# Choosing between two plans of expert slots at run time, and loading the last norm's vectors by DMA, in a hybrid encoder on one Trainium2 core

## Chip, cores and metric

The kernel runs on one core of a Trainium2 chip, as one launch. The metric is device time in microseconds, the median of several runs; lower is better. Everything below is float32, with matrix products of the dense layers split into high and low halves.

## What is computed

A trunk of two post-norm layers over 256 tokens of width 1024. Each layer has a hybrid mixer (a gated short convolution and a long convolution by Fourier transform) and then a channel mixer: dense SwiGLU in the first layer, a mixture of experts in the second. The change is in the second one's channel mixer and the norm behind it. Cut to what matters:

```python
def moe_swiglu(x, router, w1, w3, w2):          # 256 tokens, 8 experts of width 3584
    logits = xt @ router
    top_vals, top_idx = lax.top_k(logits, 2)
    top_w = jax.nn.softmax(top_vals, axis=-1)
    combine = einsum('tk,tke->te', top_w, one_hot(top_idx, 8))
    for e in range(8):
        y = y + combine[:, e:e+1] * ((silu(xt @ w1[e]) * (xt @ w3[e])) @ w2[e])

h = layer_norm(DEEPNORM_ALPHA * h + moe_swiglu(h, ...), ln_ffn_g[1], ln_ffn_b[1])
```

## The kernel before

The stream is held as 2 x 128 tokens on partitions, 1024 wide. Layer 0 and the mixer of layer 1 come first (to about 800 us); then the router, then the eight experts in a row, then the last norm and the output.

**Slots.** Only the tokens that chose an expert are computed for it. `posm` has each token's place within each expert; `one_hot` makes a matrix of tokens by slots from it, and `gather` multiplies it into the stream, which gives the expert's columns `xe`. An expert has 96 slots (wide) or 64 (narrow). Experts are taken by rank: rank 0 is always expert 0, whose key is set above all others, and the other seven follow by falling count. `vs` and `ix` hold the sorted keys and the expert numbers; SP loads the eight numbers into registers (line 1238), since the addresses of the weights depend on them. `RANKS` says which rank is computed at which place, and `N_WIDE = 5` makes ranks 0 to 4 wide: in the order of computing the experts are wide, narrow, wide, wide, narrow, wide, wide, narrow. `UNITS` says which experts share a gather. `cap` holds what each rank can take; `cmax` is how many tokens the fullest expert has beyond it. After the experts every engine loads that number (line 1266), and if it is above 0 (line 1297), `over` runs a loop over all experts for the tokens that are left.

**One expert.** `moe_run` works in four groups g of up to 1024 hidden columns. `up_proj` (matmuls on line 1054) multiplies by w1 and w3: the array is used as four column tiles of 32, a group of 32 slots in each, so 64 slots of w1 and of w3 take one PSUM bank each, and the 32 further slots of a wide expert a third bank. `gate` applies silu and the product, `turn` transposes, and `down_proj` (line 1103, and line 1108 for the further 32 slots) multiplies by w2. The down product of group g runs behind the up product of group g+1, across experts too. At the end the sum is copied from PSUM (line 1123), and `scatter` adds it to the stream `h_t`, weighted by `comb_r`. `hook` is called after each group: at group 1 it makes the next unit's one-hot matrix, at group 2 it gathers for it.

**Weights.** Each expert is 42 pieces of 1 MiB. `Weights` keeps a list of free buffers; `load` issues a DMA on SP's queue as soon as a buffer comes free, in the order of use (line 99). 16 buffers go round in the expert stage (11 named `wt`, 5 named `big`), and `W.extend` hands over a 17th, the place of `h_t`, once, in the residual ahead of the router. Because of that, `h_t` is filled with the scaled stream only in the first expert's group 1 (line 1172).

**The last norm.** `diag` builds diagonal matrices of the norm's scale and shift on POOL, `row_banks` sums them with a matrix of ones (line 523) so that every partition has the whole row, and ACT copies them out of PSUM. This happens within the last expert.

The scheduler of the framework sets the order of instructions on each engine ahead of time; instructions inside a conditional block stay inside it.

Of the kernel before, what the change touches and what calls it, by code (L numbers as in the profile page):

```python
# [33 lines left out]
RANKS = (0, 5, 1, 2, 6, 3, 4, 7)  # L34
N_WIDE = 5

UNITS = ((0,), (1, 2), (3, 4), (5,), (6, 7))
# [24 lines left out]
class Weights:  # L62
# [19 lines left out]

    def add(self, ap):

        self.src.append(ap)
# [4 lines left out]
    def load(self, upto=None):  # L90
        while self.free and self.nd < len(self.src) and (upto is None or self.nd < upto):
            a = self.free.pop(0)
            t = a[0]()
            if self.nd in self.halved:
# [119 lines left out]
def body(tc, nc, x, vec, rows, fg, winT, zT, fw1, fw2, fb, fw3, w_in, w_ao, w_ho, w_o, w13, w2,  # L214
# [105 lines left out]
    def of_rank(t, e, *q):  # L320
        if RANKS[e] == 0:
            return t[(0, *q)]
        return lambda: t[(ds(order[RANKS[e]], 1), *q)].rearrange("o p f -> (o p) f")

# [186 lines left out]

    def diag(i):

        t = big8([P, 2, KT, P])
        for q, v in enumerate((ln_g(i), ln_b(i))):
            nc.gpsimd.tensor_tensor(out=t[:, q], in0=v[:, :, None].to_broadcast([P, KT, P]),
                                    in1=id_s[:, None, :].to_broadcast([P, KT, P]), op=ALU.mult)
        return t

    def row_banks(t, q):  # L520
        banks = [acc_bank([P, 4, P]) for _ in range(2)]
        for hf in range(2):
            nc.tensor.matmul(banks[hf], ones_s, t[:, q, 4 * hf:4 * hf + 4], start=True, stop=True)
        return [b.rearrange("p k c -> p (k c)") for b in banks]
# [338 lines left out]
    for l in range(DEPTH):  # L863
# [12 lines left out]
        if l == 1:  # L876
            W.extend(lambda: hp.tile([P, 2048], F32, name="h_t", tag="h_t"), 1, False)
# [283 lines left out]
    pools = moe_pools(mctx)  # L1161
    oneh, xes, gts = {}, {}, {}

    def wide(e):
        return RANKS[e] < N_WIDE

    def hook(e, g):
        nonlocal h_t
        if e == 0 and g == 1:
            h_t = hp.tile([P, 2, D], F32, name="h_t", tag="h_t")  # L1170
            for tt in range(2):
                nc.gpsimd.tensor_scalar(out=h_t[:, tt], in0=hx[:, tt], scalar1=ALPHA, scalar2=None, op0=ALU.mult)
# [7 lines left out]
        if g == 1:  # L1180
            gts[e] = slots_T(pools, oneh.pop(e))
        if e == NE - 1 or g not in (1, 2) or unit_of(e) == unit_of(e + 1):
            return
        u = unit_of(e + 1)
        if g == 1:
            hot[u] = one_hot(pools, [(lambda tt, r=RANKS[q]: posm_r[:, tt, r:r + 1], slots(q)) for q in u])
        else:
            x = new_xe(pools, hot[u])
            for half in range(2):
                gather(x, hot[u], half)  # L1190
            hand_out(u, hot.pop(u), x)

    hot = {}

    def slots(e):
        return CAP if wide(e) else 64

    def unit_of(e):
        return next(u for u in UNITS if e in u)

    def hand_out(u, g, x):
        o = 0
        for e in u:
            oneh[e], xes[e] = g[:, :, o:o + slots(e)], x[:, :, o:o + slots(e)]
            o += slots(e)

    g0 = one_hot(pools, [(lambda tt: posm[:, tt, 0:1], CAP)])
# [3 lines left out]
    x = new_xe(pools, g0)  # L1211
    gather(x, g0, 0)
    gather(x, g0, 1)
    hand_out(UNITS[0], g0, x)
    with tc.issue_after(last["xv"].ins):

# [9 lines left out]
    def mt(shape, name, dt=F32):  # L1226
        return pools["mo"].tile(list(shape), dt, name=name, tag=name)


    cnt = rk[:, 2]  # L1230
    keys = mt([P, NE], "keys")
    nc.vector.scalar_tensor_tensor(out=keys, in0=cnt, scalar=float(NE), in1=iota_s[:, :NE], op0=ALU.mult, op1=ALU.subtract)
    nc.vector.memset(keys[:, 0:1], float(2 * NE * S))
    vs = mt([P, NE], "vs")
    ix = mt([P, NE], "ix", U32)
    nc.vector.max(out=vs, in_=keys)
    nc.vector.max_index(out=ix, in_max=vs, in_values=keys)
    for r, v in enumerate(nc.values_load_multi_w_load_instructions(ix[0:1], engines=[mybir.EngineType.SP], min_val=0,
                                                                   max_val=NE - 1)[1]):
        order[r] = v  # L1240
    perm, pick = mt([P, NE, NE], "perm"), mt([P, NE, NE], "pick")
    nc.vector.tensor_tensor(out=perm, in0=vs[:, :, None].to_broadcast([P, NE, NE]),
# [54 lines left out]
    with tc.If(count > 0):  # L1297
        over(0)
        with tc.If(count > CAP):
            over(CAP)  # L1300
# [98 lines left out]
```

## Time and profile before

| | us |
|---|---|
| median of 3 runs | 1699.12 (1696.47 to 1701.76) |
| profiled execution | 1701.1 |
| its span | 1699.3 |
| PE busy in the span | 1657.8 |
| DVE, ACT, POOL busy | 702.8, 489.5, 191.3 |
| share of 16 DMA engines, queue of the weights | 72.9% |

The span runs from the first to the last instruction of the program. A busy share is an average over stages that have different limits, so a stage is read by itself: by stretches, and by the times at which certain instructions start. PE's busy time includes matmuls whose ends are modelled. Waits, register loads and branches are not counted as busy; they are found by their lines.

### The profile page before, as it was taken

What the parts mean: (1) busy time and instruction counts of PE and PEld (TensorE: products, weight loads), DVE (VectorE), ACT (ScalarE), POOL (GpSimd) and SP (SyncE); (2) the same over time, 40 slices, a digit from 0 to 9 for tenths busy, and PEclk for the clock granted to TensorE, in tenths of its full rate; (3) what the DMA queues carried; (4) which work ended last, traced back from release to release, by engine and by line L of the source; (5) the groups of instructions that cost most, each with busy time, mean ns of one, the idle gap of its engine ahead of it and who ended that gap; (6) DMA issues with size and microseconds to landing.
All of it is one profiled execution on the core that took longest, in us unless ns stands there. A gap on an engine that the chain in (4) does not pass through costs nothing. (4 is left out here: it accounts for less than half of the span.)

```text
span 1699.3 us, 32630 instructions
## 1 busy us (share of the span) xinstructions
PE 1657.8 (98%) x14159; PEld 1081.0 (64%) x14159; DVE 702.8 (41%) x1013; ACT 489.5 (29%) x775; POOL 191.3 (11%) x163
## 2 busy tenths in 40 slices
PE   9799999999999999999999999999999999999996
PEld 7799999999998999998434333343343334434322
DVE  7789875775558898655200100101101011011102
ACT  5563575554545545542100101001001010010110
POOL 0635311030100443000010000000000000000000
PEclk9899999999999999999999999999999999999998
DMA  8442456355553536658689999999899999999993
GB/s 294 148 169 101 174 192 212 127 210 187 199 179 144 177 121 224 223 176 322 255 349 384 403 418 420 418 419 396 365 418 419 419 419 419 374 365 372 418 420 129
DMA packets 73581, 491.93 MB, mean 289 GB/s; under 512 B 8278, under 2 KB 13144, under 8 KB 14808
## 3 DMA queue, kind: packets, MB, share of 16 engines
q1 hardware_dynamic: 73000, 486.63, 72.9%
q0 software_dynamic: 432, 3.15, 0.5%
q8 instruction: 113, 1.85, 0.4%
q14 instruction: 36, 0.29, 0.0%
HBM read 488.70 MB, written 1.05 MB: 288 GB/s over the span
## 5 line engine op out<-in xcount | busy, mean ns | idle before, releaser
L1054 PE MATMUL mm<-wt,xe 128*32 128x512 f32 (+1 forms) x3664 | 473.0, 542 | 1.8 <-DMA wt<-in_m_dram 1.8
L174 PE MATMUL mm<-xh,hl 128*128 128x256 f32 x1376 | 390.7, 284 | 2.4 <-DVE t2k L747 2.3
L176 PE MATMUL mm<-xh,hl 128*128 128x256 f32 x1376 | 389.7, 283 | 2.3 <-DVE hl L168 2.3
L175 PE MATMUL mm<-xl,hl 128*128 128x256 f32 x1376 | 389.8, 283 | 0.1
L168 DVE TENSOR_TENSOR hl<-wt,hl 128x1024 fp32r<-128x1024 f32 x234 | 320.2, 1375 | 129.8 <-ACT hl L167 129.3
L1054 PE MATMUL mm<-big,xe 128*32 128x512 f32 (+1 forms) x1712 | 296.1, 535 | 0.0
L1054 PEld LDWEIGHTS mm<-wt,xe 128*32 128x32 f32 x3664 | 155.5, 110 | 214.6 <-issue 191.3
L167 ACT ACTIVATE hl<-wt 128x1024 fp32r<-128x1024 f32 x234 | 244.1, 1054 | 139.6 <-PE mm L176 74.3
L174 PEld LDWEIGHTS mm<-xh,hl 128*128 128x128 f32 x1376 | 264.1, 192 | 4.8 <-issue 2.9
L176 PEld LDWEIGHTS mm<-xh,hl 128*128 128x128 f32 x1376 | 264.0, 192 | 2.9 <-DVE hl L168 2.9
L175 PEld LDWEIGHTS mm<-xl,hl 128*128 128x128 f32 x1376 | 264.2, 192 | 1.5 <-DVE xl L168 0.7
L1064 DVE TENSOR_TENSOR act<-mm,act 128x512 f32<-128x512 f32 (+1 forms) x32 | 20.0, 625 | 486.4 <-PE mm L1054 486.4
L1103 PE MATMUL acc<-wt,at 128*32 128x512 f32 x1232 | 192.8, 593 | 0.0
L1054 PEld LDWEIGHTS mm<-big,xe 128*32 128x32 f32 x1712 | 86.3, 110 | 101.2 <-issue 90.5
L1063 ACT ACTIVATE act<-mm 128x512 f32<-128x512 f32 (+1 forms) x32 | 17.4, 544 | 459.9 <-PE mm L1054 459.9
L493 POOL TENSOR_TENSOR rs<-rs,mhalf 128x1 f32<-128x1 f32 x10 | 6.8, 676 | 1065.2 <-DVE rs L492 1065.2
L1103 PEld LDWEIGHTS acc<-wt,at 128*32 128x32 f32 x1232 | 53.2, 110 | 83.7 <-issue 81.7
L1103 PE MATMUL acc<-big,at 128*32 128x512 f32 x544 | 101.5, 593 | 0.6 <-DMA big<-in_m_dram 0.6
L1108 PE MATMUL acc<-wt,bt 128*32 128x512 f32 x352 | 100.2, 592 | 0.0
L174 PE MATMUL mm<-big,hl 128*128 128x256 f32 x256 | 72.3, 282 | 0.0
L176 PE MATMUL mm<-big,hl 128*128 128x256 f32 x256 | 72.3, 282 | 0.0
L175 PE MATMUL mm<-big,hl 128*128 128x256 f32 x256 | 72.3, 282 | 0.0
(251 smaller groups left out, 1803.0 us busy)
## 6 DMA issues: line engine op xcount, KB each, us to landing
wt<-in_m_dram SPq DMA_DIRECT2D x231, 1024.0 KB, 13.1
big<-in_m_dram SPq DMA_DIRECT2D x103, 1024.0 KB, 14.0
wt<-in_w_in_dram SPq DMA_DIRECT2D x62, 1024.0 KB, 4.8
wt<-in_w_dram SPq DMA_DIRECT2D x33, 1024.0 KB, 4.8
wt<-in_w_ho_dram SPq DMA_DIRECT2D x8, 1024.0 KB, 4.9
wt<-in_w_ao_dram SPq DMA_DIRECT2D x7, 1024.0 KB, 4.9
wt<-in_w_o_dram SPq DMA_DIRECT2D x6, 1024.0 KB, 4.9
big<-in_rows_dram POOLq DMA_DIRECT2D x3, 1024.0 KB, 5.6
```

The costliest lines, as they stand in the source:

```text
L167: a = nc.scalar.activation(hi, src, AF.Copy)
L168: v = nc.vector.tensor_tensor(out=lo, in0=src, in1=hi.bitcast(F32), op=ALU.subtract)
L174: nc.tensor.matmul(out, ah, bh, start=start, stop=False)
L175: nc.tensor.matmul(out, ah, bl, start=False, stop=False)
L176: nc.tensor.matmul(out, al, bh, start=False, stop=stop)
L493: last["pow"] = nc.gpsimd.tensor_tensor(out=rs, in0=rs, in1=mhalf[:, 0:1], op=ALU.pow)
L1054: nc.tensor.matmul(banks[r][32 * q:32 * q + 32, :n], xe[:, k, 32 * sg:32 * sg + 32], cols(w, b, q4), start=k == 0, stop=k == KT - 1, tile_ ...
L1063: nc.scalar.activation(a[:, :n], banks[0][:, :n], AF.Silu)
L1064: nc.vector.tensor_tensor(out=a[:, :n], in0=banks[1][:, :n], in1=a[:, :n], op=ALU.mult)
L1103: nc.tensor.matmul(ya[32 * q:32 * q + 32], at[:, f, 64 * b + 32 * sg:64 * b + 32 * sg + 32], ch[b][0][:, h * D + db * 512:h * D + (db + 1) ...
L1108: nc.tensor.matmul(yb[32 * q:32 * q + 32], bt[:, f, 32 * b:32 * b + 32], ch[b][0][:, h * D + db * 512:h * D + (db + 1) * 512], start=first ...
```

## The change

The one static plan is replaced by two. `LEAN` has ranks 1 to 4 wide and four narrow experts, expert 0 among them; `FULL` has ranks 0 to 5 wide. The number `lost`, how many tokens the fullest expert of `LEAN` would lose, is worked out ahead of the experts and loaded by every engine; `tc.If(lost < 1)` chooses. Each branch holds its own copy of the whole expert stage (`experts`) and its own copy of the state of the weights (`fork`); the test for left-over tokens and the loop `over` are now inside the `FULL` branch only. The first expert's gather stands ahead of the branch, into a buffer of the `big` pool; the weighting of tokens (`comb`) and the sorting of `posm` and `comb` by rank move behind it. `h_t` is no longer lent as a weight buffer. `diag` and `row_banks` go; the last norm's two vectors are read from HBM into every partition by a DMA on POOL's queue, into another buffer of `big`. The sort key of an expert is 8 times its count less its number, so no two are equal.

```diff
-RANKS = (0, 5, 1, 2, 6, 3, 4, 7)
-N_WIDE = 5
-UNITS = ((0,), (1, 2), (3, 4), (5,), (6, 7))
+LEAN = {"ranks": (0, 1, 5, 2, 6, 3, 4, 7), "wide": (1, 2, 3, 4), "units": ((0,), (1, 2), (3, 4), (5,), (6, 7))}
+FULL = {"ranks": (0, 6, 1, 2, 7, 3, 4, 5), "wide": (0, 1, 2, 3, 4, 5), "units": ((0,), (1, 2), (3, 4), (5,), (6,), (7,))}
...
+    def fork(self):
+
+        w = Weights(self.tc, self.nc, None, None, 0, 0)
+        w.src, w.raw, w.free = self.src, dict(self.raw), list(self.free)
+        w.nd, w.nu, w.whole, w.halved = self.nd, self.nu, self.whole, self.halved
+        return w
...
-        if l == 1:
-            W.extend(lambda: hp.tile([P, 2048], F32, name="h_t", tag="h_t"), 1, False)
...
+    x0 = big8([P, KT, S])[:, :, :CAP]
+    gbf = big8([P, 2, D])
...
+    def without(name, n, keep0):
+
+        cap = mt([P, NE], f"cap{name}")
+        nc.vector.tensor_scalar(out=cap, in0=keys, scalar1=vs[:, n:n + 1], scalar2=float(CAP - 64), op0=ALU.is_ge, op1=ALU.mult)
+        if not keep0:
+            nc.vector.memset(cap[:, 0:1], 0.0)
+        rest = mt([P, NE], f"rest{name}")
+        nc.vector.scalar_tensor_tensor(out=rest, in0=cnt, scalar=-64.0, in1=cap, op0=ALU.add, op1=ALU.subtract)
+        cmax, cmi = mt([P, 1], f"cmax{name}"), mt([P, 1], f"cmi{name}", I32)
+        nc.vector.reduce_max(out=cmax, in_=rest, axis=mybir.AxisListType.X)
+        nc.vector.tensor_scalar(out=cmax, in0=cmax, scalar1=0.0, scalar2=None, op0=ALU.max)
+        nc.vector.tensor_copy(cmi, cmax)
+        return cap, nc.values_load(cmi[0:1, 0:1], min_val=0, max_val=S)
+
+    lost = without("l", 4, False)[1]
+    nc.vector.max_index(out=ix, in_max=vs, in_values=keys)
+    gather(x0, g0, 0)
+    gather(x0, g0, 1)
...
-        if e == 0 and g == 1:
-            h_t = hp.tile([P, 2, D], F32, name="h_t", tag="h_t")
...
-        if e == NE - 1 and g == 0:
-            gb["diag"] = diag(N_LN - 1)
-        if e == NE - 1 and g == 2:
-            gb["last"] = big8([P, 2, D])
-            for q in range(2):
-                for hf, b in enumerate(row_banks(gb["diag"], q)):
-                    nc.scalar.activation(gb["last"][:, q, hf * 512:(hf + 1) * 512], b, AF.Copy)
...
+            if e == NE - 2 and g == 0:
+                src = rows[N_LN - 1]
+                nc.gpsimd.dma_start(gbf, bass.AP(tensor=src.tensor, offset=src.offset, ap=[[0, P], [D, 2], [1, D]]))
...
-    count = nc.values_load(cmi[0:1, 0:1], min_val=0, max_val=S)
...
-    with tc.If(count > 0):
-        over(0)
-        with tc.If(count > CAP):
-            over(CAP)
...
+    with tc.If(lost < 1) as plan:
+        with ExitStack() as pctx:
+            experts(LEAN, W.fork(), moe_pools(pctx))
+    with plan.Else():
+        with ExitStack() as pctx:
+            pools = moe_pools(pctx)
+            W1 = W.fork()
+            experts(FULL, W1, pools)
+
+            cap, count = without("f", 5, True)
+            with tc.If(count > 0):
+                over(pools, W1.free, cap, 0)
+                with tc.If(count > CAP):
+                    over(pools, W1.free, cap, CAP)
```

How instructions move, at three places. On PE, between the gather for the first expert and its first up products, before:

```order
L1009 MATMUL acc<-oneh,xh 128x96 x16
L1054 MATMUL mm<-big,xe 32x512 x4
L1054 MATMUL mm<-wt,xe 32x512 x4
L1054 MATMUL mm<-big,xe 32x512 x2
L1054 MATMUL mm<-wt,xe 32x512 x2
```

and now:

```order
L1002 MATMUL acc<-oneh,xh 128x96 x16
L1187 TENSOR_LOAD cmil
L1287 COMPARE_AND_BRANCH
L1047 MATMUL mm<-big 32x512 x4
L1047 MATMUL mm<-wt,big 32x512 x4
```

A register load and the branch (`cmil` is the number `lost`) stand between the two, and the up products read the gathered columns from a `big` buffer.

On SP, the weights that are issued ahead of the routing and the first ones behind it, before:

```order
L99 DMA wt<-in_m_dram 128x2048 x8
L99 DMA h_t<-in_m_dram 128x2048
L1238 TENSOR_LOAD ix
L1238 ISA x16
L1266 TENSOR_LOAD cmi
L1266 ISA x2
L99 DMA big<-in_m_dram 128x2048 x2
```

and now:

```order
L108 DMA wt<-in_m_dram 128x2048 x8
L1193 TENSOR_LOAD ix
L1187 TENSOR_LOAD cmil
L1287 COMPARE_AND_BRANCH
L108 DMA big<-in_m_dram 128x2048 x2
```

The load into `h_t` is gone, and the branch stands ahead of the first load that needs a buffer of the expert stage.

On POOL, from the norm ahead of the router to the end, before:

```order
L516 TENSOR_TENSOR big<-vec_s,id_s 128x1024 x2
L1218 TENSOR_TENSOR ew<-eb,ew 128x2
L1219 TENSOR_SCALAR ew<-ew 128x2
L1172 TENSOR_SCALAR h_t<-xh 128x1024 x2
L1266 TENSOR_LOAD cmi
L1297 COMPARE_AND_BRANCH
```

and now:

```order
L1187 TENSOR_LOAD cmil
L1287 COMPARE_AND_BRANCH
L1221 TENSOR_SCALAR h_t<-xh 128x1024
L1241 TENSOR_TENSOR ew<-eb,ew 128x2
L1221 TENSOR_SCALAR h_t<-xh 128x1024
L1242 TENSOR_SCALAR ew<-ew 128x2
L1224 DMA big<-in_rows_dram 128x2048
L1287 UNCONDITIONAL_BRANCH
```

The scaling of the stream (`h_t`) now stands ahead of and between the two steps of the tokens' weights (`ew`), the diagonals are gone, and the DMA of the norm's vectors is the next thing behind them.

## Rows read from the trace of the kernel before

**Rows 1.** The page, part 2: the TensorE clock granted, in tenths, 40 slices of 42.5 us.
```profile
PEclk9899999999999999999999999999999999999998
```

**Rows 2.** Timeline of PE, 818 to 822: start us, us, engine, line, operation, count.
```profile
818.62 1.06 PE L1054 MATMUL mm<-big,xe 128*32 128x512 f32 x8
```

**Rows 3.** Timeline of ACT: the first copies out of PSUM that end each expert.
```profile
950.96 1.21 ACT L1123 ACTIVATE y<-acc 64x512 f32<-64x512 f32 x2 [4.53 <-PE acc L1103]
...
1041.25 1.21 ACT L1123 ACTIVATE y<-acc 64x512 f32<-64x512 f32 x2 [2.84 <-PE acc L1103]
...
1163.97 1.21 ACT L1123 ACTIVATE y<-acc 64x512 f32<-64x512 f32 x2 [3.69 <-PE acc L1103]
...
1277.17 1.21 ACT L1123 ACTIVATE y<-acc 64x512 f32<-64x512 f32 x2 [2.93 <-PE acc L1103]
...
1372.35 1.21 ACT L1123 ACTIVATE y<-acc 64x512 f32<-64x512 f32 x2 [2.83 <-PE acc L1103]
...
1495.07 1.21 ACT L1123 ACTIVATE y<-acc 64x512 f32<-64x512 f32 x2 [3.69 <-PE acc L1103]
...
1608.28 1.21 ACT L1123 ACTIVATE y<-acc 64x512 f32<-64x512 f32 x2 [2.93 <-PE acc L1103]
...
1680.41 1.21 ACT L1123 ACTIVATE y<-acc 64x512 f32<-64x512 f32 x2 [10.02 <-PE acc L1103]
```

**Rows 4.** Timeline of PE in the first expert: eight instructions a row.
```profile
821.22 1.04 PE L1054 MATMUL mm<-big,xe 128*32 128x512 f32 x8
822.08 1.04 PE L1054 MATMUL mm<-wt,xe 128*32 128x512 f32 x8
```

**Rows 5.** Groups by form: the second down line, wide experts alone; count, busy us, ns.
```profile
L1108 PE MATMUL acc<-wt,bt 128*32 128x512 f32 x352 | 100.2, 592 | 0.0
...
L1108 PE MATMUL acc<-big,bt 128*32 128x512 f32 x200 | 68.3, 592 | 0.0
```

**Rows 6.** Stretches: length, busy us of PE, PEld, DVE, ACT, POOL, clock, DMA share, GB/s.
```profile
829.00:951.00 122.00, 121.91 (x1198) 43.88 (x1194) 9.02 (x19) 8.77 (x18) 5.52 (x2) 1.00 0.93 369
...
951.00:1041.00 90.00, 86.89 (x832) 30.59 (x824) 8.59 (x13) 7.50 (x14) 0.00 (x0) 1.00 1.01 419
...
1164.00:1277.00 113.00, 112.22 (x1084) 43.38 (x1084) 11.37 (x19) 9.45 (x18) 0.00 (x0) 1.00 0.95 390
...
829.00:1670.00 841.00, 830.54 (x7934) 316.11 (x7930) 82.76 (x146) 71.64 (x136) 5.52 (x2) 1.00 0.97 399
...
1670.00:1680.00 10.00, 10.00 (x96) 2.86 (x88) 0.00 (x0) 0.38 (x1) 0.00 (x0) 1.00 0.01 2
```

**Rows 7.** Line 523, the row sums of the diagonals: duration ns min/median/max, starts.
```profile
L523 PE MATMUL acc<-big,cst_s x8: 592/594/697, 1629.9 to 1637.2; 128*128 128x512 f32 x8
```

**Rows 8.** Lines 1266 and 1297, the test at the end: duration ns, starts us.
```profile
L1266 PEldq EVENT_SEMAPHORE  x6: 51/51/51, 1684.8 to 1685.3; - x6
...
L1266 PEldq TENSOR_LOAD <-cmi x1: 491/491/491, 1685.4 to 1685.4; - x1
...
L1297 PEldq COMPARE_BRANCH  x1: 3455/3455/3455, 1686.0 to 1686.0; - x1
...
L1297 DVEq COMPARE_BRANCH  x1: 72/72/72, 1687.3 to 1687.3; - x1
```

**Rows 9.** Timeline of SP's queue ahead of and behind the routing.
```profile
801.04 0.33 SPq L99 DMA_DIRECT2D h_t<-in_m_dram  x1
...
829.14 0.81 SPq L99 DMA_DIRECT2D big<-in_m_dram  x2
```

**Rows 10.** Tile h_t on POOL: duration ns min/median/max, starts.
```profile
L1172 POOL TENSOR_SCALAR h_t<-xh x2: 2765/2776/2786, 867.4 to 870.2; 128x1024 f32<-128x1024 f32 x2
```

**Rows 11.** The page, part 6: issues, KB each, us to landing.
```profile
wt<-in_w_in_dram SPq DMA_DIRECT2D x62, 1024.0 KB, 4.8
...
big<-in_rows_dram POOLq DMA_DIRECT2D x3, 1024.0 KB, 5.6
```

**Rows 12.** Timeline of DVE: the last norm begins; idle us ahead of it, releaser.
```profile
1687.97 1.88 DVE L488 BATCH_NORM_STATS2 st<-h_t 128x6 f32<-128x512 f32 x3 [0.65 <-DVEq L1297]
```

More of the change, by code (lines that the diff above doesn't have):

```diff
@@ L1160, in body, with mt @@
     mctx = ExitStack()
[L1161 to L1168, printed above, removed]
-        if e == 0 and g == 1:
-            h_t = hp.tile([P, 2, D], F32, name="h_t", tag="h_t")
-            for tt in range(2):
-                nc.gpsimd.tensor_scalar(out=h_t[:, tt], in0=hx[:, tt], scalar1=ALPHA, scalar2=None, op0=ALU.mult)
-        if e == NE - 1 and g == 0:
-            gb["diag"] = diag(N_LN - 1)
-        if e == NE - 1 and g == 2:
-            gb["last"] = big8([P, 2, D])
-            for q in range(2):
-                for hf, b in enumerate(row_banks(gb["diag"], q)):
-                    nc.scalar.activation(gb["last"][:, q, hf * 512:(hf + 1) * 512], b, AF.Copy)
[L1180 to L1207, printed above, removed]
+    first = {"mo": mctx.enter_context(tc.tile_pool(name="mo0", bufs=1))}
+    def mt(shape, name, dt=F32, pool=first):
+        return pool["mo"].tile(list(shape), dt, name=name, tag=name)
+    g0 = one_hot(first, [(lambda tt: posm[:, tt, 0:1], CAP)])
     with tc.issue_after(last["oneh"].ins), tc.issue_after(cp.ins):
@@ L1210, in body @@
             ins = h_half(tt, 1, back[tt])
[L1211 to L1215, printed above, removed]
+    x0 = big8([P, KT, S])[:, :, :CAP]
+    gbf = big8([P, 2, D])
+    cnt = mt([P, NE], "cnt")
+    nc.vector.tensor_copy(cnt, rk[:, 2])
+    keys = mt([P, NE], "keys")
+    nc.vector.scalar_tensor_tensor(out=keys, in0=cnt, scalar=float(NE), in1=iota_s[:, :NE], op0=ALU.mult, op1=ALU.subtract)
+    nc.vector.memset(keys[:, 0:1], float(2 * NE * S))
@@ new lines, in body, with experts, wide, slots @@
+    lost = without("l", 4, False)[1]
+    nc.vector.max_index(out=ix, in_max=vs, in_values=keys)
+    gather(x0, g0, 0)
+    gather(x0, g0, 1)
+    for r, v in enumerate(nc.values_load_multi_w_load_instructions(ix[0:1], engines=[mybir.EngineType.SP], min_val=0,
+                                                                   max_val=NE - 1)[1]):
+        order[r] = v
+    def experts(plan, W, pools):
+        ranks, units = plan["ranks"], plan["units"]
+        order["plan"] = plan
+        oneh, xes, gts, hot = {}, {}, {}, {}
+        posm_r, comb_r = mt([P, 2, NE], "posm_r", pool=pools), mt([P, 2, NE], "comb_r", pool=pools)
+        def wide(e):
+            return ranks[e] in plan["wide"]
+        def slots(e):
+            return CAP if wide(e) else 64
+        def unit_of(e):
+            return next(u for u in units if e in u)
+        def hand_out(u, g, x):
+            o = 0
+            for e in u:
+                oneh[e], xes[e] = g[:, :, o:o + slots(e)], x[:, :, o:o + slots(e)]
+                o += slots(e)
+        def hook(e, g):
+            if e == 0 and g == 1:
+                for tt in range(2):
+                    nc.gpsimd.tensor_scalar(out=h_t[:, tt], in0=hx[:, tt], scalar1=ALPHA, scalar2=None, op0=ALU.mult)
+            if e == NE - 2 and g == 0:
+                src = rows[N_LN - 1]
+                nc.gpsimd.dma_start(gbf, bass.AP(tensor=src.tensor, offset=src.offset, ap=[[0, P], [D, 2], [1, D]]))
+            if g == 1:
+                gts[e] = slots_T(pools, oneh.pop(e))
+            if e == NE - 1 or g not in (1, 2) or unit_of(e) == unit_of(e + 1):
+                return
+            u = unit_of(e + 1)
+            if g == 1:
+                hot[u] = one_hot(pools, [(lambda tt, r=ranks[q]: posm_r[:, tt, r:r + 1], slots(q)) for q in u])
+            else:
+                x = new_xe(pools, hot[u])
+                for half in range(2):
+                    gather(x, hot[u], half)
+                hand_out(u, hot.pop(u), x)
+        hand_out(units[0], g0, x0)
@@ L1237, in body @@
[L1237 to L1242, printed above, removed]
-                            in1=keys[:, None, :].to_broadcast([P, NE, NE]), op=ALU.is_equal)
```

68 lines of the change are left out of this document (21 added, 47 removed).

## The prediction

> **What bounds the kernel now.** The granted TensorE clock is full almost everywhere [rows 1], so the clock is no term. I first read where the expert stage begins and ends. The first expert matmul starts at 818.62 us [rows 2]; each expert ends with the first copy of its sum out of PSUM, eight rows in all [rows 3], the last at 1680.41; the tail from there to the end of the span (1699.3) is 18.9 us. So 862 of 1699 us are the expert stage, and nearly all of the change lies there.
>
> Then I asked who is the limit in it. Two resources are nearly even. **PE:** eight instructions (four column tiles, two passes each; a "unit") take 822.08 - 821.22 = 0.86 us [rows 4]. By the code a wide expert has 24 x 3 units of 512 columns and 8 x 3 half units up, and 14 x 3 down: 126 units; a narrow one has 84. The third that a wide one has more is 42 units, which the count of the second down line bears out: 552 instructions are 5 experts x 14 units x 8, a few records short [rows 5]. **DMA:** every expert brings 42 MiB. In the narrow expert's stretch the queue moves 419 GB/s, share 1.01, thus 2.50 us a MiB and 105 us an expert; in a wide one it falls to 390, in the first to 369, since no buffer is free [rows 6]. Over 829 to 1670 the mean is 399 GB/s. At 420 the same 335.6 MB would have taken 799 us, so 42 us of the queue were lost behind PE. Expert-to-expert times say the same [rows 3]: wide followed by wide 122.7 us, wide followed by narrow 113.2, narrow followed by wide 90.3, or 95.2 where a gather for the next unit lies in it; the first, wide, took 132.3 from 818.62. Wide ones are over the DMA's 105, narrow ones under it, and 16 MiB of buffers smooth it. PE is the limit through most of the stage.
>
> **Which plan runs.** The reference's own inputs send 61, 61, 71, 69, 67, 64, 53 and 66 assignments to the experts. Expert 0 has 61; the four largest others are 71, 69, 67, 66; the rest are 64, 61, 53. All fit (64 and 96 slots), the 64 with nothing to spare, so `lost` is 0 and the plan with four wide experts runs.
>
> **The change, part by part.**
> (a) Expert 0 becomes narrow and the order is now N W N W N W W N. 42 units x 0.857 = 36.0 us less on PE. To see whether the weights keep up I add up expert by expert, with the measured interval of the same kind. The first has 84 + 24 units to its end where it had 126 + 16: 132.3 - 34 x 0.857 = 103.2. Then 113.2, 95.2, 113.2, 95.2, 122.7, 113.2 (gathers stand in the same units as before, after the first, third, fifth and sixth expert).
> (b) The diagonal matrices and their row sums go: eight matmuls of 512 columns [rows 7], 8 x 0.43 = 3.4 us at PE's pace, at most 8 x 0.59 = 4.8; I take 4. They stood in the last expert, so 72.1 becomes 68.1. ACT and POOL lose work that nobody waited for.
> (c) The branch. On PE it is a TENSOR_LOAD behind the gather and a compare, and all expert matmuls are queued behind it. The same pair at the end of the kernel costs PE 0.49 us for the load and up to six 0.05 us waits ahead of it; the DVE compare took 0.07, but the jump that PE took there 3.46 [rows 8]. The lean plan is the fall-through, so I take 1.2 us: PE starts at 819.8. Bounds: 0 (the load runs while the gather drains) and 3.5. SP does its loads while no buffer is free and pays nothing: its queue stands from 801 to 829 [rows 9]. On DVE the chain of the largest count now comes ahead of the copies of x0; it is the one that stood there for the end's test, cost nothing then, and is in the 1.2 now.
> (d) POOL now scales the residual at the branch, 2 x 2.78 us [rows 10], ahead of the step that DVE's reciprocal waits for; the gates queue behind that reciprocal. 819.8 + 5.6 + about 3 for the small steps is 828.4; the first gate is due at 819.8 + 16 x 0.857 = 833.5. Hidden, with 5 us of cover; if it is gone, the excess is PE's.
> (e) h_t no longer takes the 17th MiB ahead of time [rows 9], and the last norm's rows come as 1 MiB on POOL's queue, right behind the reciprocal's step. Both go through the same 16 engines: 2 x 2.50 us if the DMA is the limit, 0 if PE is. Landing took 5.6 us and is needed 800 us later [rows 11].
>
> **The DMA beside it.** The first four buffers come free after 8 units instead of 12: 829.1 - 3.4 + 1.2 = 827. A lone MiB lands in 4.8 us [rows 11]. When the first expert ends, 50 MiB must be there, 16 were, one more is (e)'s: 831.8 + 34 x 2.5 = 916.8; then 105 each. PE alone against DMA alone: 923.0/916.8, 1036.2/1021.8, 1131.4/1126.8, 1244.6/1231.8, 1339.8/1336.8, 1462.5/1441.8, 1575.7/1546.8, 1643.8/1631.8. PE is later everywhere, by 3 to 29 us, under the 40 us that 16 buffers hold. But in the first, third and fifth expert the cover is 3 to 6 us, and weights are used in lumps of four; there PE will wait. I take 3 us in all; bounds 0 and 12 (4 at each).
>
> **The end.** DVE's idle 0.65 us ahead of the last norm [rows 12] is the test of the count, which goes. In its place DVE jumps over the general plan. The order has 79 instructions of DVE under the jump before and 266 now; DVE's jump before took 0.07 us, PE's, over 1229, took 3.46 [rows 8]. Between -0.65 and +2.9 I take 0: the distance is nearer to DVE's row. The Trainium skill ("Runtime: NRT & Kernel Launch", Instruction fetch mechanics) says that an engine fetches instructions in blocks of 256, and that a taken branch whose target lies outside the two blocks it holds has to wait for a DMA. The trace agrees on both jumps; by that rule this one may fall either way, and the time would be 1668.4 if it falls out.
>
> **Sum.** PE's end 1643.8 + 3 = 1646.8, tail 18.9: span 1665.7, where it was 1699.3. The profiled execution is 1.8 us longer than its span, 1701.1, and 2.0 above the median of 1699.1. So 1701.1 - 33.6 = 1667.5 for that execution, **1665.5** for the median. Another way: 36.0 + 4 - 1.2 - 3 = 35.8 less, thus 1663.3.
>
> **The rivals.**
> *Weights late.* The narrow experts starve and the DMA still idles behind the pair of wide ones. For it: both resources are within 1% of each other above. If half of the 42 us are lost again, the last MiB lands at 1631.8 + 21, and with the 10.4 us that PE had left after the DMA fell still [rows 6, 3] the span is 1682; time 1682. If all are lost again, 1703: no change. Against: the three stretches that lost most are the first wide one and the two pairs of wide ones, of which one pair is left.
> *The general plan runs* (the change doesn't do what it says). One assignment more at the expert with 64 decides it. Then six are wide, W N W W N W W W: 132.3 + 90.3 + 122.7 + 113.2 + 95.2 + 122.7 + 122.7 + 97.2 (68.1 + 34 units) = 896.3; with 819.8, 18.9 and 1.2 for the second test the span is 1736 and the time **1736**, slower. Against: the router's second and third logit differ by at least 0.0047 on every token in the reference, and no token near that would join that expert.
> *The branch is dear.* Every engine fetches anew at the entry and the end: 3.5 - 1.2 + 2.9 = 5.2 more, 1670.7. Inside the range.
>
> **How the numbers follow.** The sum's case, with the bounds of (b), (c), waits and jump, runs from 1658 to 1680: 0.82. Late weights, half: 0.10. Late weights in full, no change: 0.03. The general plan: 0.05. The range 1657 to 1682 leaves out the last two and part of the others. About 0.3%, 5 us, is what a measurement can tell from no change: faster 0.92, same 0.03, slower 0.05.
>
> **What would show it.** Eight endings with the first near 923, the last near 1647, and only 8/10 of the second down line's instructions (4 x 112 = 448); an SP queue that begins again near 827; the DMA share at 1.01 for all but the sixth and seventh expert; the first expert matmul at 819 to 821; a DVE gap ahead of the last norm of under 1 us or near 3.5. Wrong: over 660 instructions in that line (general plan), a first gate later than 836 (POOL's chain), or PE waits on weights over 12 us in sum.

## The result, and the profile after

The changed kernel took 1672.35 us (median of 4 runs, 1671.37 to 1673.24), beside 1698.61 for the kernel before on the same chip (1696.47 to 1701.76): ratio 0.9844, interval 0.9827 to 0.9861. The forecast was 1665.5, range 1657 to 1682. By the medians the gain is 26.3 us. Profiled execution against profiled execution it is 1672.95 (span 1671.2) where 1701.1 (span 1699.3) was: 28.1 us less by the spans, and 33.6 were forecast. So the direction came, and 5.5 us of the gain did not.

The eight endings of the experts stand in the timeline of ACT, as in [rows 3] (start us, us, engine, line, operation):

```profile
923.77 1.21 ACT L1116 ACTIVATE y<-acc 64x512 f32<-64x512 f32 x2 [2.85 <-PE acc L1096]
...
1035.90 1.21 ACT L1116 ACTIVATE y<-acc 64x512 f32<-64x512 f32 x2 [2.93 <-PE acc L1096]
...
1133.86 1.21 ACT L1116 ACTIVATE y<-acc 64x512 f32<-64x512 f32 x2 [2.85 <-PE acc L1096]
...
1245.94 1.21 ACT L1116 ACTIVATE y<-acc 64x512 f32<-64x512 f32 x2 [2.93 <-PE acc L1096]
...
1346.15 1.21 ACT L1116 ACTIVATE y<-acc 64x512 f32<-64x512 f32 x2 [2.84 <-PE acc L1096]
...
1468.91 1.21 ACT L1116 ACTIVATE y<-acc 64x512 f32<-64x512 f32 x2 [3.69 <-PE acc L1096]
...
1582.11 1.21 ACT L1116 ACTIVATE y<-acc 64x512 f32<-64x512 f32 x2 [2.93 <-PE acc L1096]
...
1650.99 1.21 ACT L1116 ACTIVATE y<-acc 64x512 f32<-64x512 f32 x2 [10.02 <-PE acc L1096]
```

They were forecast at 923.0, 1036.2, 1131.4, 1244.6, 1339.8, 1462.5, 1575.7, 1643.8. The intervals between them say more: 112.1, 98.0, 112.1, 100.2, 122.8, 113.2, 68.9. The two narrow experts in the middle, third and fifth, were to take 95.2 each. They took 2.8 and 5.0 more; the rest is within 2 us.

Where the stage begins (timeline of PE, as [rows 2]; the first row is the gather ahead of the branch):

```profile
815.18 3.71 PE L1002 MATMUL acc<-oneh,xh 128*128 128x96 f32 x32
818.82 1.06 PE L1047 MATMUL mm<-big 128*32 128x512 f32 x8
```

The first expert matmul starts at 818.82, where it was 818.62; the gather too is 0.2 later than before (814.98). The branch cost nothing at the entry. Which plan ran is read from the second down line, groups by form, as [rows 5]:

```profile
L1101 PE MATMUL acc<-wt,bt 128*32 128x512 f32 x288 | 76.8, 592 | 0.0
...
L1101 PE MATMUL acc<-big,bt 128*32 128x512 f32 x160 | 46.7, 592 | 0.0
```

448 = 4 x 112: four wide experts. The stretches (length; busy us of PE, PEld, DVE, ACT, POOL; clock; DMA share; GB/s), as [rows 6]:

```profile
829.00:938.00 109.00, 108.38 (x1016) 40.42 (x1009) 6.58 (x11) 10.89 (x19) 0.00 (x0) 1.00 1.01 420
...
1251.00:1347.00 96.00, 89.90 (x825) 32.56 (x824) 7.36 (x13) 6.21 (x13) 0.00 (x0) 1.00 1.01 419
1347.00:1467.00 120.00, 119.21 (x1152) 49.12 (x1154) 12.34 (x24) 9.51 (x19) 0.00 (x0) 1.00 1.00 411
1467.00:1579.00 112.00, 111.22 (x1076) 43.22 (x1072) 11.37 (x19) 9.30 (x18) 0.00 (x0) 1.00 0.96 393
...
829.00:1640.00 811.00, 795.93 (x7538) 304.74 (x7530) 76.94 (x132) 68.29 (x128) 0.00 (x0) 1.00 1.00 414
```

The queue moves 414 GB/s over the stage where it moved 399. It is at its pace up to the fifth expert and falls below it in the sixth (411) and the seventh (393), as forecast. It begins again at 825.06 (SP's queue, as [rows 9]; 827 was forecast):

```profile
825.06 0.83 SPq L108 DMA_DIRECT2D big<-in_m_dram  x2
```

The end, as [rows 12] (timeline of DVE; idle us in brackets):

```profile
1655.82 2.07 DVE L1134 SCALAR_TENSOR_TENSOR h_t<-mm,comb_r,h_t 128x512 f32<-128x512 f32 x3 [0.53 <-PE mm L1133]
1659.77 1.88 DVE L497 BATCH_NORM_STATS2 st<-h_t 128x6 f32<-128x512 f32 x3 [1.88 <-issue]
```

The compares of the branch, at the entry and at the jump behind the plan, as [rows 8] (line 1287: duration ns min/median/max, first and last start):

```profile
L1287 PEldq COMPARE_BRANCH  x2: 92/1920/3747, 817.8 to 1655.5; - x2
...
L1287 DVEq COMPARE_BRANCH  x2: 51/53/55, 819.9 to 1656.8; - x2
```

DVE's idle 0.65 us ahead of the last norm became 1.88: it jumps over the general plan. The compare that is put down for it takes only 0.05, but from it (1656.8) to the first instruction behind the jump (1659.8) it is 3.0 us; for 1.1 of them the last step of the scatter (the first row), already issued, still runs. PE's jump at the end takes 3.75 us, but nobody waits for PE there.

### The profile page after: what moved, and what is told of

It is laid out like the page before. It is cut to its first block, busy times and chain, and to the rows that moved or that the text cites. A ratio compares the mean times of both kernels' runs of the same rounds, so it can differ in the third digit from the quotient of the medians.

```text
span 1671.2 us, 31810 instructions
## 1 busy us (share of the span) xinstructions
PE 1621.3 (97%) x13769; PEld 1068.1 (64%) x13769; DVE 699.0 (42%) x1004; ACT 484.7 (29%) x766; POOL 188.3 (11%) x162
## 4 chain that ended last, share of the span: by engine, by line
PE 77%; DVE 9%; DMA 8%; ACT 2%; issue 2%; POOL 2%; SPq 0%; DVEq 0%; POOLq 0%; ACTq 0%
PE mm L1047 26%; PE acc L1096 10%; PE mm L183 8%; PE mm L184 8%; PE mm L185 8%; DMA wt<-in_m_dram 7%; DVE hl L177 3%; PE acc L1101 3%; PE acc L183 2%; PE acc L184 2%; PE acc L185 2%; PE acc L1002 1%; DVE big L177 1%; PE tp L1072 1%; PE mm L253 1%
## 5 line engine op out<-in xcount | busy, mean ns | idle before, releaser
L1047 PE MATMUL mm<-wt,xe 128*32 128x512 f32 (+1 forms) x3184 | 363.6, 541 | 0.5 <-DMA wt<-in_m_dram 0.5
L1047 PEld LDWEIGHTS mm<-wt,xe 128*32 128x32 f32 x3184 | 126.6, 110 | 194.8 <-issue 174.1
L1047 PE MATMUL mm<-big,xe 128*32 128x512 f32 (+1 forms) x1424 | 199.2, 538 | 1.3 <-DMA big<-in_m_dram 1.3
L1096 PE MATMUL acc<-wt,at 128*32 128x512 f32 x1200 | 178.5, 593 | 0.3 <-DMA wt<-in_m_dram 0.3
L1047 PEld LDWEIGHTS mm<-big,xe 128*32 128x32 f32 x1424 | 64.4, 110 | 74.9 <-issue 61.6
L1096 PE MATMUL acc<-big,at 128*32 128x512 f32 x592 | 95.9, 594 | 1.3 <-DMA big<-in_m_dram 1.3
L1101 PE MATMUL acc<-wt,bt 128*32 128x512 f32 x288 | 76.8, 592 | 0.0
```

The lines of the kernel that those rows point to most:

```text
L1047: nc.tensor.matmul(banks[r][32 * q:32 * q + 32, :n], xe[:, k, 32 * sg:32 * sg + 32], cols(w, b, q4), start=k == 0, stop=k == KT - 1, tile_ ...
L1096: nc.tensor.matmul(ya[32 * q:32 * q + 32], at[:, f, 64 * b + 32 * sg:64 * b + 32 * sg + 32], ch[b][0][:, h * D + db * 512:h * D + (db + 1) ...
L1101: nc.tensor.matmul(yb[32 * q:32 * q + 32], bt[:, f, 32 * b:32 * b + 32], ch[b][0][:, h * D + db * 512:h * D + (db + 1) * 512], start=first ...
```

## Experiments

Times of stages are best compared from the first expert matmul on, since everything ahead of it drifts by up to 1 us between executions. From there the changed kernel's last ending comes after 1650.99 - 818.82 = 832.2 us. All runs are beside the kernel before on the same chip.

**The norm's rows, late.**

```diff
+                with tc.issue_after(last["xv"].ins):
                     nc.gpsimd.dma_start(gbf, ...)
```

> The only edit: the DMA of the last norm's rows waits for the gather that the sixth expert makes, so its 1 MiB passes near 1440 us and not at 824. Theory A (weights are the limit to the fifth expert's end; DMA share 1.01 there): 1 MiB less ahead of it is 2.5 us, the fifth expert ends near 1343.7 (changed kernel 1346.15), the eighth near 1648.5 (1650.99), time near 1670. Theory B (PE with its gathers and lumps is the limit there): the endings stay within 0.5 us, time 1672.

1672.02 us, ratio 0.9842 (0.9825 to 0.9858). The timeline of POOL shows that the edit did not do what it says:

```profile
823.53 0.64 POOL L1225 DMA_DIRECT2D big<-in_rows_dram  x1
```

The transfer went out at 823.53, as early as before: the edit asks for a place in the list of instructions, and on POOL nothing stands ahead of it. So this is a second sample of the changed kernel and decides nothing; all eight endings agree with the first sample's within 0.1 us, counted from the first expert matmul (817.96).

**Five wide experts in the new frame.**

```diff
-LEAN = {"ranks": (0, 1, 5, 2, 6, 3, 4, 7), "wide": (1, 2, 3, 4), ...
+LEAN = {"ranks": (0, 5, 1, 2, 6, 3, 4, 7), "wide": (0, 1, 2, 3, 4), ...
```

> The lean plan gets the five wide experts and the order of the kernel before; branch, rows by DMA and the unlent h_t stay. Theory A (the gain is the 42 units of expert 0; the other parts give 4 us for the row sums and take 1.2 at the end): the first expert ends near 951, the last near 1677, time 1694 to 1698. Rival (the gain comes from the row sums, the earlier scaling of h_t or the new layout, and the narrow expert only starves): time 1672 to 1685.

1697.56 us, ratio 0.9991 (0.9982 to 1.0001). All the other parts together are worth 1.3 us, and their interval reaches no change; the fourth narrow expert is worth 25.2 us. The time that it spared PE was put at 36.0.

**No branch.** `LEAN` alone, no test, no general plan.

> The lean plan alone, with no branch and no general plan (left out: what happens when a token finds no slot). Theory A (the entry costs nothing, the jump at the end 1.2 us): the eight endings stay within 0.5 us, DVE's idle ahead of the last norm falls from 1.88 us to under 0.3, time about 1.5 us less, near 1671. Rival (the branch also costs inside the stage, by the order of instructions that the scheduler can't mix across it, or by code fetched twice): the endings move by 2 us or more.

1671.94 us, ratio 0.9839 (0.9823 to 0.9855). The branch as a whole costs 0.4 us, within what runs differ by, but this is a sum of two signs: the endings come 1.0 to 3.1 us later, as the rival said, and DVE's idle time ahead of the last norm is gone, as theory A said. The end is 2.1 us shorter (18.1 us from the last ending to the end of the span, where the changed kernel has 20.2). The start is 3.1 later (timeline of DVE, timeline of PE, and the columns of a stretch):

```profile
815.00 0.17 DVE L1242 RECIPROCAL ew<-ew 128x2 f32<-128x2 f32 x1 [1.82 <-POOL ew L1241]
...
815.82 0.17 DVE L974 SCALAR_TENSOR_TENSOR posm<-tp,mask 128x16 f32<-128x16 f32 x1
```

```profile
816.56 5.44 PE L1002 MATMUL acc<-oneh,xh 128*128 128x96 f32 x32 [1.73 <-DVE oneh L989]
821.92 1.06 PE L1047 MATMUL mm<-big 128*32 128x512 f32 x8
```

```profile
818.00:820.00 2.00, 2.00 (x12) 2.00 (x11) 1.90 (x8) 0.06 (x1) 2.00 (x1) 0.50 0.00 0
```

Without the branch the small steps of the gate weights move ahead of the routing in the list. DVE's reciprocal waits for POOL, which scales the residual for 2.80 us first, and `posm`, which the first gather needs, is queued behind the reciprocal. It is the wait that step (d) named, at another place: the branch keeps it behind the gather. Behind PE's idle 1.73 us the granted clock also falls to half (0.50 in the stretch shown, where the changed kernel has 1.00), and the gather takes 5.44 where it took 3.71. By the last ending only 1.0 of the 3.1 is left: the fifth expert waits less.

**The last norm inside both plans,** so that no engine jumps ahead of it.

```diff
+            last_norm()
     with plan.Else():
...
+            last_norm()
```

> The last norm and the stores are written into both plans, so DVE jumps after them and not before. Theory A (1.88 us of idle are the fetch behind the jump): the idle ahead of the norm falls under 0.3 us, the jump is paid beside the stores' landing, time 1.2 to 1.7 us less, near 1671. Rival (the jump is paid in full wherever it stands, since the closing barrier waits for every engine): the idle goes and the time stays at 1672.4, with a gap of 2 us or more behind the last store.

1674.93 us, ratio 0.9857 (0.984 to 0.9873). That is 2.6 us slower than the changed kernel, which neither theory said. DVE's idle time goes, and the stores start 2.3 us earlier (1662.25, where 1664.51 was); but the span ends at 1673.1, where it ended at 1671.2. Now SP jumps, behind the stores (lines 1299 and 1187: duration ns, first and last start):

```profile
L1299 SPq COMPARE_BRANCH  x2: 38/46/53, 818.0 to 1666.1; - x2
...
L1187 SPq FUSED_REGOPS  x1: 169/169/169, 1668.9 to 1668.9; - x1
```

Its compare is at 1666.1 and its next instruction 2.8 us later, at 1668.9; register operations behind the branch follow to 1671.6. In the changed kernel the same jump lies at 1625.4, 39 us ahead of the first store, and costs nothing. A jump is paid where its engine is the one that is waited for.

**The plans exchanged,** so that the jump comes at the entry.

```diff
-    with tc.If(lost < 1) as plan:
-        experts(LEAN, ...)
-    with plan.Else():
-        experts(FULL, ...)
+    with tc.If(lost > 0) as plan:
+        experts(FULL, ...)
+    with plan.Else():
+        experts(LEAN, ...)
```

> The two plans change places in the branch: the general plan stands first and the lean one is the other arm. Every engine now jumps at the entry over the general plan, and none jumps at the end. Theory A: a jump at the entry costs PE what its jump at the end cost, 3.75 us, and PE cannot hide it, since all expert matmuls stand behind it: first expert matmul at 822.2 to 822.6 instead of 818.82; DVE's idle 1.88 us ahead of the last norm goes; net +1.7, median 1674.1. Theory B: the jump hides behind the gather of the first unit: first expert matmul within 0.5 us of 818.8 and only the gain at the end is left, 1670.5.

1672.38 us, ratio 0.9842 (0.9826 to 0.9859): the same time, from two parts. The entry (timeline of PE, then two stretches) and the end (timeline of DVE):

```profile
815.36 3.71 PE L1002 MATMUL acc<-oneh,xh 128*128 128x96 f32 x32
821.95 1.74 PE L1047 MATMUL mm<-big 128*32 128x512 f32 x8 [2.88 <-issue]
```

```profile
822.00:824.00 2.00, 2.00 (x12) 0.65 (x16) 0.97 (x6) 0.00 (x0) 0.83 (x2) 0.55 0.08 16
824.00:826.00 2.00, 2.00 (x16) 0.70 (x12) 1.60 (x5) 0.00 (x0) 2.00 (x1) 0.60 0.00 0
```

```profile
1659.57 1.87 DVE L497 BATCH_NORM_STATS2 st<-h_t 128x6 f32<-128x512 f32 x3
```

The jump costs PE 2.88 us of idle time, and behind it the granted clock is 0.55 and 0.60 in two stretches of 2 us, a mixture of its two levels (1.2 and 2.4 GHz), where it is 1.00 in the changed kernel. The first ending comes 4.8 us later. So PE can't hide the jump, as theory A said, though the jump itself is shorter than its 3.75 us and the clock adds 1.7; theory A's time, 1674.1, did not come. The fifth expert then waits less for weights (98.4 us), so the last ending is only 2.8 later. At the end DVE has no idle time, and 3.0 us come back: 17.2 us to the end of the span. Not all of that is the jump. Behind the last ending PE waits 1.85 us for ACT in both runs, and then the granted clock falls: in the changed kernel within the next stretch of 2 us (1652.99 to 1654.99: 0.58), here later (1655.83 to 1657.83: 1.00), so the last scatter ends 6.9 us behind the last ending there and 5.8 here. This 1.1 comes and goes between executions (in the run with the late rows, a second sample of the changed kernel, the scatter ends after 5.9); the jump is the other 1.9, DVE's gap in the changed kernel. What the jump costs at one end it spares, nearly, at the other.

**Orders.** The pair of wide experts earlier:

```diff
+LEAN: N W N W W N W N   (units 0 / 1,2 / 3 / 4,5 / 6,7)    order a
+LEAN: N W W N W N W N   (units 0 / 1 / 2,3 / 4,5 / 6,7)    order b
```

> Lean order N W N W W N W N instead of N W N W N W W N; nothing else changes. Theory A (the narrow third and fifth experts waited for weights, 2.8 and 5.0 us, because they come when the queue is only some 6 us ahead): the pair of wide ones now comes as fourth and fifth and builds up cover before the next narrow one, so only the third still waits 2.8; intervals 112, 98, 122.7, 113.2, 95.2 or less, 113.2, 68 to 69; last ending about 1646.3, 4.7 us earlier than 1650.99, median 1667.7. Theory B (each narrow expert in the middle loses these microseconds by its own gathers and copies, wherever it stands): the sixth expert takes 98 to 100 us, the last ending stays at 1650 to 1651, median 1672.4. Theory C (the queue as a whole is the limit by now): last ending 1646 at best and the last landing at 1638, whatever PE does.

> Lean order N W W N W N W N. Theory A: the pair of wide ones comes second and third, and no narrow expert stands where the queue is short of cover; intervals 122.7, 113.2, 90 to 95, 113.2, 95.2, 113.2, 68.1; PE alone would end at 1643.5, the queue without a pause at 1638.2 for the last landing and so 1646.1 for the last ending (7.9 us from last landing to last ending as now): median 1667.5. Theory B: fourth and sixth take 98 to 100, median 1672.4. Theory D: the wide pair comes so early that all buffers fill and the queue pauses, which costs later: DMA share below 0.97 in the second or third expert, later narrow ones wait again, median 1671 to 1674.

Order a: 1669.75 us, ratio 0.9828 (0.9811 to 0.9844), last ending 829.6 us after the first expert matmul. Order b: 1669.30, ratio 0.9824 (0.9807 to 0.984), 828.9. Both gain about 3 us, and less than theory A said: the sixth expert, narrow, takes 97.9 us in both, near theory B's 98, though the last ending did not stay. The reason is in order b's fourth expert, narrow, with the last MiB that it needs landing 15.7 us ahead of its ending (at 1241.66, by the trace's record of the transfers; timeline of ACT):

```profile
1159.55 1.21 ACT L1116 ACTIVATE y<-acc 64x512 f32<-64x512 f32 x2 [2.93 <-PE acc L1096]
...
1257.37 1.21 ACT L1116 ACTIVATE y<-acc 64x512 f32<-64x512 f32 x2 [2.83 <-PE acc L1096]
```

1257.37 - 1159.55 = 97.8 us with only four short waits for weights, 1.1 us in sum: the same as the third expert of the changed kernel, in which no weight load waited for a DMA. So its 2.8 us are explained without the queue. What the two have in common is the gather for a unit of two experts, 160 columns. The third expert of the changed kernel against the fifth of the kernel before (groups by form, line of the gather; count, busy us, ns, idle):

```profile
L1002 PE MATMUL acc<-oneh,xh 128*128 128x160 f32 x32 | 5.7, 315 | 0.7 <-DVE oneh L989 0.7
...
L1002 PEld LDWEIGHTS acc<-oneh,xh 128*128 128x128 f32 x32 | 4.5, 189 | 4.3 <-issue 2.5 <-DVE oneh L989 1.0 <-ACT xe L1006 0.8
```

```profile
L1009 PE MATMUL acc<-oneh,xh 128*128 128x96 f32 x32 | 4.3, 282 | 0.4 <-DVE oneh L996 0.4
...
L1009 PEld LDWEIGHTS acc<-oneh,xh 128*128 128x128 f32 x32 | 3.8, 191 | 2.3 <-issue 1.7 <-DVE oneh L996 0.6
```

160 columns cost 1.4 us more of matmuls and 2.0 more of idle time ahead of their weight loads. The 95.2 us came from an expert with a gather of 96 columns. Order a shows that the queue stands just behind: its third expert gathers only 96 columns and takes 97.7 us all the same, now with 3.8 us of waits for weights. Theory D is borne out in part: the queue pauses at the early wide pair (1049 to 1142: 383 GB/s), but the next narrow expert, the sixth, doesn't take longer for it (97.9 us).

**The general plan, always.**

```diff
-    with tc.If(lost < 1) as plan:
+    with tc.If(lost < 0) as plan:
```

> The test is made so that the general plan always runs (six wide, two narrow, then its own test of the count, which finds nothing over). Theory A, the rival as the prediction priced it: eight intervals 132.3, 90.3, 122.7, 113.2, 95.2, 122.7, 122.7, 97.2, time 1736. Theory B: PE's taken jump at the entry comes on top, 3.7 us: 1740. Theory C: with six wide ones the queue always has cover and PE takes less than its measured intervals: below 1731.

1735.20 us (1734.44 to 1735.90), ratio 1.0214 (1.0197 to 1.0231). Theory A, the rival's sum of 1736, within 1 us. The page has no compare at that line (presumably since a count below 0 can't be, and the test is folded away), so this run says nothing of the entry's jump. It is what the changed kernel costs where one token more comes to an expert than the lean plan has slots, less the jump at the entry, which would come on top as in the exchanged plans.

**Gathers in the wide experts,** the order kept.

```diff
-"units": ((0,), (1, 2), (3, 4), (5,), (6, 7))
+"units": ((0,), (1,), (2, 3), (4, 5), (6, 7))
```

> The order of the changed kernel, but the gathers for the next unit lie in the wide experts (units 0 / 1 / 2,3 / 4,5 / 6,7), so that the narrow third and fifth carry none. Theory A (the queue is the limit up to the fifth expert; a narrow one ends 5.9 us after its last weights land, however little PE has to do): third and fifth still end near 1133.9 and 1346.2, nothing is gained, median 1671.5 to 1672.8; PE's waits for weights grow by what the gathers took. Theory B (the third expert's 2.8 us over the forecast are its own gather of 160 columns, 97.9 us against 95.2 with 96 columns, and PE's time counts): third and fifth shorter by 7 to 10 us, median about 1660.

1671.73 us, ratio 0.9837 (0.9821 to 0.9854): theory A. Third and fifth expert end 315.0 and 527.3 us after the first expert matmul, as in the changed kernel, to 0.1 us. What PE was spared went into waiting for weights, 18.9 us in all, where the changed kernel has 9.0 (waits of the weight loads over the stage: us, times, longest):

```profile
PEld mm L1047 <- DMA wt<-in_m_dram: 6.5, 10, 2.3
PEld acc L1096 <- DMA wt<-in_m_dram: 4.5, 7, 1.6
PEld mm L1047 <- DMA big<-in_m_dram: 4.5, 4, 2.2
...
PEld acc L1096 <- DMA big<-in_m_dram: 3.4, 4, 2.3
```

So two limits stood one on the other in the third expert: PE with its gather, and the queue, which would have let it end no earlier.

**A 17th MiB ahead, and the rows truly late.**

```diff
     gbf = big8([P, 2, D])
+    W.extend(lambda: gbf.rearrange("p a d -> p (a d)"), 1, False)
...
+                nc.vector.tensor_copy(gbf[:, 0, 0:1], xes[e][:, 0, 0:1])
                 src = rows[N_LN - 1]
```

> The buffer of the norm rows holds a 17th MiB of weights first, loaded with the others before the stage, and the rows come only when the seventh expert begins (a copy of one column from its gathered tokens into that buffer holds them back). Theory A (the two MiB of term (e) cost the queue's pace as long as the queue is the limit): every landing up to the fifth expert comes 2.5 us earlier against the first expert matmul; rows of the fifth expert's waits fall from 8.4 us of weight-load idle time to under 6; last ending 2.5 earlier, median 1669.9. Theory B (PE is the limit again by the end, and the queue was late only in passing): no change, 1672.4.

1668.04 us (1667.74 to 1669.14), ratio 0.9817 (0.9801 to 0.9834), the fastest of all. The fifth and the last ending (timeline of ACT), and the waits of the weight loads over the stage:

```profile
1341.31 1.21 ACT L1116 ACTIVATE y<-acc 64x512 f32<-64x512 f32 x2 [2.85 <-PE acc L1096]
...
1646.52 1.21 ACT L1116 ACTIVATE y<-acc 64x512 f32<-64x512 f32 x2 [10.02 <-PE acc L1096]
```

```profile
PEld mm L1047 <- DMA wt<-in_m_dram: 2.6, 5, 1.3
...
PEld mm L1047 <- DMA big<-in_m_dram: 1.3, 2, 1.0
...
PEld acc L1096 <- DMA wt<-in_m_dram: 1.0, 4, 0.3
...
PEld acc L1096 <- DMA big<-in_m_dram: 0.6, 2, 0.3
```

The 17th MiB goes out at 805.41, and the rows at 1414.6. The last ending comes 828.0 us after the first expert matmul (818.50), 4.15 us less than 832.2, where theory A expected 2.5: the edit moves both MiB of step (e), and the landings up to the fifth expert are 4.3 to 4.5 us earlier by the same count, nearly two MiB at 2.5. Waits for weights fall from 9.0 us to 5.5. This is the price of step (e), and most of what the forecast missed.

**Order b with the gathers in the wide experts, and both together.**

> Order N W W N W N W N with the gathers in the wide experts (units 0 / 1 / 2 / 3,4 / 5,6 / 7). PE's intervals by the rows so far: 104, 122, 115, 88, 115, 88, 115, 69, some 12 us less than in the same order with gathers in the narrow ones. Theory A (floor of the queue): 319 MiB from 832 on at 2.527 us, last landing 1638.2, last ending 7.9 behind it, 1646: median 1667. Theory B (PE counts): last ending 1636, median 1657. Theory C (gathers cost the same wherever they lie): 1669.3 as with this order before.

> Both edits together: order N W W N W N W N, gathers in the wide experts, a 17th MiB of weights ahead and the norm rows late. Theory A (floor of the queue): 318 MiB from 832 on, 2.5 us less than with the order and the gathers alone, about 1664.5. Theory B (PE is the limit): the same time as without the 17th buffer.

The first took 1669.50 us (ratio 0.9826, 0.9809 to 0.9842), the last ending after 828.3 us: 0.6 less than order b alone. A gather of 160 columns costs a wide expert less than a narrow one: the third, wide, takes 117.6 us with it and 113.2 without, the fourth, narrow, 90.5 without and 97.8 with it. But this plan has six units instead of five, so one gather more, of 64 columns, lies in the seventh expert: it takes 116.4 us where order b has 112.1, with 0.5 us of waits for weights. And the queue pauses in the third expert (1049 to 1142: 380 GB/s), and the last one, with 5.5 us of waits for weights, takes 70.7 us instead of 68.9. These two take back nearly all that the narrow experts gain. The time is theory C's, but not for its reason.

The second took 1671.33 (0.9835, 0.9818 to 0.9851): 3.3 us slower than the 17th MiB alone and 1.8 slower than the order alone (there the runs overlap), against both theories. The 17th MiB's lead is lost in the third expert, where all buffers are full (366 GB/s in the same stretch), and the rows go out in the fifth, when the queue is the limit (timeline of POOL):

```profile
1325.56 0.64 POOL L1226 DMA_DIRECT2D big<-in_rows_dram  x1 [500.91 <-POOLq L1289]
```

The last landing that the fifth expert needs comes 4.2 us later than without the 17th MiB, counted from the first expert matmul, and the sixth expert, narrow, takes 94.6 us instead of 90.4. The rows' own MiB is 2.4 us of this; the other 1.8 are there already at the fourth expert's last landing, and why is not shown. Here a lead was worth what it kept until the first wait, and it kept nothing through a stretch in which the queue stood.

## Why the prediction was right, and where it fell short

Added up in its own terms, from the first expert matmul on:

| step | forecast us | measured us |
|---|---|---|
| first expert | 103.2 | 104.95 |
| second and fourth | 2 x 113.2 | 2 x 112.1 |
| third | 95.2 | 98.0 |
| fifth | 95.2 | 100.2 |
| sixth, seventh | 122.7, 113.2 | 122.8, 113.2 |
| last, (b) in it | 68.1 | 68.9 |
| waits for weights, in all | 3 | in the rows above |
| stage | 827.0 | 832.2 |
| (c) start | 819.8 | 818.8 |
| tail | 18.9 | 20.2 |
| span | 1665.7 | 1671.2 |

The start, 1.0 us early, and the tail, 1.3 late, nearly cancel, which is luck; the stage is the miss.

**(a)** The mechanism is right: one wide expert less, and the run with five wide ones shows that nearly the whole gain is this. Its size failed at two points of the sum. The interval 95.2 was taken for both narrow experts "where a gather for the next unit lies in it", whatever the gather's width: with 160 columns it is 98.0, and order b shows that with hardly a wait for weights. And **"I take 3 us in all"** was too little: the fifth expert alone took 5.0 us over its 95.2, with the gather of 96 columns that the 95.2 has. The waits of its weight loads, 8.4 us in sum, not all of which holds up the matmuls:

```profile
PEld acc L1096 <- DMA big<-in_m_dram: 2.9, 2, 2.2
PEld mm L1047 <- DMA big<-in_m_dram: 2.9, 2, 2.2
...
PEld mm L1047 <- DMA wt<-in_m_dram: 1.4, 1, 1.4
PEld acc L1096 <- DMA wt<-in_m_dram: 1.2, 1, 1.2
```

The prediction held PE's ending against the last landing and called 3 to 6 us "cover". But PE works 5.9 us more between that landing and the ending (1340.22 to 1346.15; in the third 1127.92 to 1133.86; the landings are from the trace's record of the transfers), so a cover of 3 us is a wait of 3 us. The run with the gathers in the wide experts bears this out: there too third and fifth end 5.9 us behind their landings. The landings themselves were late by 1.1 us for the third and 3.4 for the fifth: an expert's 42 MiB take 106.15 us, not 105 (the stretch between two such landings):

```profile
1234.07:1340.22 106.15, 100.01 (x924) 34.84 (x920) 9.43 (x16) 8.43 (x16) 0.00 (x0) 1.00 1.01 419
```

419 GB/s in 106.15 us are 0.44 MB more than 42 MiB. The trace puts 0.13 MB of that down to the queues that fetch instructions; what the rest is stays open. 1340.2 + 5.9 gives the measured ending. The first expert's 1.75 us over the forecast are no wait for weights, for none of its weight loads waited for a DMA; their cause stays open.

**(b)** 3.2 us of the 4 forecast (72.1 to 68.9).

**(c)** The entry cost 0, not 1.2; the register load (488 ns at 817.2) ran while the gather drained, the lower bound. The exchanged plans, which jump there, pay 2.88 us and 1.7 more by the clock, over the upper bound of 3.5.

**(d)** Hidden, as forecast, and sooner:

```profile
817.86 2.80 POOL L1221 TENSOR_SCALAR h_t<-xh 128x1024 f32<-128x1024 f32 x1 [13.92 <-DVE big L1004]
...
821.34 2.79 POOL L1221 TENSOR_SCALAR h_t<-xh 128x1024 f32<-128x1024 f32 x1
...
824.38 0.64 POOL L1224 DMA_DIRECT2D big<-in_rows_dram  x1
```

POOL had done with the reciprocal's step at 824.4, forecast 828.4, and the first gate's activation began at 833.4, behind its table load; it was due at 833.5.

**(e)** The rows' DMA stands in the last of these rows. I counted the two MiB at 2.5 us each if the queue is the limit, and then put PE behind the queue everywhere, so that they weighed little. Both are worth 4.15 us together, by the run with the 17th MiB: the fifth ending comes 4.5 us earlier, as much as the landings do, and the last expert takes 0.4 longer. That is most of the 5.2 us that the stage took over the forecast. (The first expert is 1.0 shorter in that run too, without a wait for weights in either; since the fifth ending goes by the landings, this adds nothing to it.)

**The end.** DVE's gap is 1.88 us, where the text gave under 1 or near 3.5: 1.2 more than before, and 0 was taken. By the rule of the Trainium skill that the prediction weighed ("Runtime: NRT & Kernel Launch", Instruction fetch mechanics), the jump went out of the blocks that DVE held. The runs agree in so far as the jumps over the general plan cost 2.8 us or more from the compare to the next instruction (DVE 3.0, SP 2.8, PE's compare alone 3.75 and 3.85), the compares that fall through 0.04 to 0.09. So "nearer to DVE's row" was the wrong choice: a jump over 266 instructions cost DVE nearly what the bound took from PE's row, and the gap is shorter only since the scatter's last step still ran for 1.1 us of it.

**The rivals.** Weights late in half was too dark: the queue paused in the sixth and seventh expert only. Its direction was right, as the fifth expert shows. The general plan did not run; its price was right to 1 us. The branch was not dear.

## What to carry to other kernels

When two resources are nearly even, do not compare their ends: add to the last landing the work that still has to be done on it, and count every transfer that a change adds as time until the queue first pauses. An interval borrowed from another place must have the same side work in it, here the width of a gather. In a branch, look which engine is waited for behind each jump: there a jump cost 1.9 us (DVE at the end), 2.8 (SP behind the stores) or 4.6 (PE at the entry, 1.7 of it by the clock), and elsewhere nothing. Which arm stands first made no difference to the time here, since the arm that falls through at the entry jumps at the end.

## What the runs showed that was not expected

A jump's price is not in the compare's row on every engine: DVE's compare took 0.05 us with 3.0 us to the next instruction behind the jump, of which work already issued hid 1.1; SP's took 0.04 with 2.8; PE's row holds the whole 3.75. An idle PE paid twice: after 2.88 us (the exchanged plans) and after 1.73 us (no branch) without work its granted clock was near half for 3 to 4 us, worth 1.7 us each time. Behind the last expert the same idle time was followed by a fall of the clock sooner in one execution and later in another, which moves the end by 1.1 us. A lead of one MiB in a queue that had a pause ahead was worth nothing in the one order that tried it. Why the same gather costs a narrow expert 7.3 us and a wide one 4.4 was not tried.
